# Weights of a hybrid attention and expert layer, laid out by the host as contiguous chunks of 1 MB

## The chip, the core and the metric

The kernel runs on one core of a Trainium2 chip. Its time is the time on the device, in microseconds (us), as the median of several runs. Matrix products run on TensorE (PE in the profile; PEld is its load of the stationary operand), elementwise work on VectorE (DVE) and ScalarE (ACT), a little on GpSimd (POOL). SyncE (SP) issues the loads, and 16 DMA engines carry them from HBM into SBUF, whose 128 partitions are the rows of every tile.

## What is computed

One decoder layer over 256 tokens of width 1024, in float32, with 256 memory tokens:

```python
proj = einsum('bsd,de->bse', rmsnorm(x, attn_norm_g), w_in)   # 1024 x 2320: three groups of heads
o_gla  = silu(gla_r) * rmsnorm(gla_chunked(q, k, v, forget_gate))
o_moba = moba_attention(qnorm(q), knorm(k), v, alibi_slopes)  # one block of 256: causal softmax
o_mem  = memory_attention(qnorm(q), *split(rmsnorm(mem) @ w_mem_kv))
x = x + concat(o_gla, o_moba, o_mem) @ w_out
h = rmsnorm(x, ffn_norm_g)
# experts: best of 4 groups, best 2 of its 8 experts; 32 experts of width 512
x = x + sum(gate[e] * ((silu(h @ w_gate[e]) * (h @ w_up[e])) @ w_down[e]) for e in chosen)
```

The projections w_in, w_mem_kv and w_out have some 16 MB, the weights of the 32 experts 192 MB (1 MB is 1,048,576 bytes where chunks are meant).

## The kernel before

All weights go through buffers of 1 MB, 128 partitions of 8 KB: a ring of 21 (`RING`), of which the attention part keeps some for its own data, and two more (`LATE`) later. A chunk of weights fills one buffer and is one DMA, issued by SP in the helper `chunk` (L93). The program's order of loads is the order on SP's queue; a load waits until the products that read its buffer's former contents are done.

**Attention part.** `load_chunk` loads 16 chunks: 512 columns of a projection by half of its eight k-tiles, so a partition gets four rows of 512 columns. They are issued in the order of the list `loads`, among small loads (gains, biases, router weights). The work on them follows one long list, `order`, in which every engine's instructions stand in fixed order: `w` splits a k-tile of weights in two float32r parts (ACT and DVE), `mm` multiplies.

**Experts.** `batch` runs over eight batches of four experts, each expert with 32 slots for tokens. A batch takes 24 chunks: four steps c of w_gate and w_up, each in two halves of two experts (`wNg`, `wNu` in the profile, N the batch), then eight chunks of w_down (`wNd`). A gate or up chunk has two k-rows of 512 columns for each of two experts: the k-rows of a partition are neighbours in HBM, since row d = 8 p + i of an expert lies on partition p. A down chunk has a row of 1024 columns for each of two experts. The last batch's down chunks are cut by columns, in order that output can leave earlier: four of 512 columns for one expert each, then four of 256 columns for two experts. Products: `pgate` and `pup` (L988), `pdn` (L1001, or L51 in the last batch, where a helper issues them), `acc` and `pc_b` for adding gated outputs to their tokens, `pg_b` for gathering tokens.

`prefetch(n)` puts the next n loads on SP's queue; `batch` calls it until the chunk that it needs is issued. Before batch 2 the kernel issues 20 loads ahead, then enters a loop over overflowing experts (`overflow`, L1086), which has no turns when, as here, no expert gets more than 32 tokens:

```python
for b in range(NB):
    if b == 1:
        overflow_blocks()
    if b == 2:
        prefetch(RING - 1)
        overflow()
    batch(b, final=(b == NB - 1))
```

Of the kernel before, what the change touches and what calls it, by code (L numbers as in the profile page):

```python
# [8 lines left out]
F32 = mybir.dt.float32  # L9
# [10 lines left out]
T = 256            # tokens  # L20
NT = T // P        # token tiles
D = 1024
KD = D // P        # k-tiles over the model width: row d = 128 * i + p, or 8 * p + i for the experts
FF = 512
KF = FF // P       # k-tiles over the expert width
NE = 32            # experts
EB = 4             # experts of one batch, one column group of the tensor engine each
C = 32             # slots of an expert in a batch
NB = NE // EB
NBLK = 16          # most blocks of 128 that assignments past slot C can fill  # L30
EPS = 1e-6
BIG = 1e30
RING = 21          # buffers of 1 MB: weight chunks in flight, and what the attention part keeps
LATE = 2           # more of them, once the attention part is done
H4 = 4             # heads of each group
SLOPES = [2.0 ** (-8.0 * (h + 1) / H4) for h in range(H4)]


class InOrder:
    """An engine whose instructions are issued in the order of the program."""  # L40
# [16 lines left out]
def layer(tc, x, mem, attn_norm_g, mem_norm_g, w_in, w_gla_gk, b_gla_gk, gla_out_norm_g,  # L57
          moba_q_norm_g, moba_k_norm_g, w_mem_kv, mem_q_norm_g, mem_k_norm_g, w_out,
          ffn_norm_g, w_router_group, b_router_group, w_router_expert, b_router_expert,
          w_gate, w_up, w_down, out):  # L60
    nc = tc.nc
    with ExitStack() as ctx:
# [5 lines left out]
        # in the order in which others want the space  # L68
# [18 lines left out]
        def chunk(src, name, shape, v=None):  # L87
            v = slot(name) if v is None else v
            if len(shape) == 2:
                v = v.rearrange("p (a b) -> p a b", a=shape[0])  # L90
            else:
                v = v.rearrange("p (a b c) -> p a b c", a=shape[0], b=shape[1])
            load(out=v, in_=src)  # L93
            return v

        # ---------------------------------------------------------------- loads and constants
# [5 lines left out]
        # what the attention part keeps, in buffers that hold weights later  # L102
# [17 lines left out]
        # gains and biases, as rows of 128 at first  # L120
# [6 lines left out]
        wkv = w_mem_kv[0].rearrange("(i p) e -> p i e", p=P)  # L127
        wo = w_out[0].rearrange("(i p) e -> p i e", p=P)
        columns = {"o": (wo, 0), "qk": (win, 0), "v": (win, 512), "r": (win, 1024), "mb": (win, 1552), "e": (win, 2064), "kv": (wkv, 0)}
        chunks = {}  # L130

        def load_chunk(name, h):
            """512 columns of a projection, half of its k-tiles; the output projection has columns twice that."""
            src, c = columns[name]
            c += 512 * (h // 2)
            chunks[name, h] = chunk(src[:, 4 * (h % 2):4 * (h % 2) + 4, c:c + 512], f"w_{name}{h}", (4, 512))
# [3 lines left out]
        # router weights (rows d = 512 * q + 4 * p + j) and bias; columns 4..7 pad the group logits to the 8 that max  # L140
        # takes
# [10 lines left out]
        def load_small(what):  # L152
# [11 lines left out]
            elif what == "qk gains":  # L164
                # for both heads of a pair
# [38 lines left out]
        # ---------------------------------------------------------------- attention part  # L204
# [8 lines left out]
        def split(src, hi, lo):  # L213
            """src as the sum of two float32r parts, exactly; products of them in three passes have float32's
            accuracy."""
            act.copy(hi, src)
            dve.tensor_tensor(lo, src, hi.bitcast(F32), op=ALU.subtract)
# [6 lines left out]
        def norm(src, r, name):  # L224
            """1 / rms of rows."""
            junk = work.tile([P, D], BF16, name="junk_" + name, tag="w2")
            ss = small.tile([P, 1], F32, name="ss_" + name, tag="ss")
            act.activation(junk, src, AF.Square, accum_out=ss)
            rstd_of(ss, 1, D, name, r)

        def norm_T(xh, t, q, dst, name):
            """Half of the columns, transposed and split: dst[part][q, i, token]."""
# [5 lines left out]
        def head_norm(ps, rx, n, name):  # L238
            """QK-norm, without the gains, of the n heads of 64 in ps times rx."""
# [10 lines left out]
        def heads_T(qn, t, n, g0, dst, name):  # L250
            """With the gains, transposed by head pairs into dst."""
# [16 lines left out]
        def softmax(sc, n, name, rl=None):  # L268
            """Softmax over the n keys of each head (sc: by head parity, [P, head pair, n])."""
# [22 lines left out]
        def softmax_T(ex, n, name):  # L292
            """Transposed: [key, key tile, head, query]."""
# [19 lines left out]
        # ---- the normalised rows  # L313
# [10 lines left out]
        def constants(what):  # L324
# [5 lines left out]
            elif what == "rel":  # L330
                # distance i - j of query i of the last tile to key j, huge where the key is later
# [3 lines left out]
            elif what == "amask":  # L335
                # key j (partition) of the same 64-chunk as query i and not later
# [7 lines left out]
        def more_constants():  # L344
# [3 lines left out]
            # strictly earlier tokens, and all tokens  # L348
# [17 lines left out]
        # ---- the projections in pieces: a k-tile of 512 columns  # L366
        weights, banks, passed = {}, {}, {}

        def w(name, n):
            """Splits the weights of piece n, with the gains of the norm before them."""  # L370
# [10 lines left out]
        def sums(name, n):  # L381
            """The bank, and whether this is the first, or the last, of the eight k-tiles that it sums."""
# [6 lines left out]
        def mm(name, n, t):  # L389
            """Piece n's products: rows of token tile t times 512 columns; for qk transposed, feature tiles 2 t and  # L390
            2 t + 1 by tokens; for the output projection, k-tile n % 8 of the mixed heads times columns of half n // 8."""
# [17 lines left out]
        # ---- what goes on between the pieces  # L409
        # MoBA and memory  # L410
# [19 lines left out]
        def go(key, f, *args):  # L430
            """The next part of a computation that goes on over several pieces; state keeps what it yields."""
# [44 lines left out]
        def rx_T(part):  # L476
            """The tokens' 1 / rms along the columns."""
# [36 lines left out]
        # GLA  # L514
# [4 lines left out]
        def lr_proj():  # L519
# [4 lines left out]
            # the sums over both parts of the weights, which the next product adds  # L524
# [53 lines left out]
        def inside():  # L578
            """Inside a chunk: masked products of queries and keys, transposed."""
# [11 lines left out]
        def states(part):  # L591
            """The states before chunks 1..3: products, then sums."""
# [70 lines left out]
        # ---- the last of the output projection, residual, FFN norm, router logits  # L663
# [101 lines left out]
        # ---- routing: top-1 group, top-2 experts in it  # L765
# [28 lines left out]
        # place of each assignment in its expert's list (from 1; 0 where the expert isn't chosen), and the  # L794
        # one-hot rows of the first batch
# [20 lines left out]
        def keep_warm(n):  # L816
            """Products that nobody reads: the array's clock halves when it idles."""
# [22 lines left out]
        # gate weight: softmax of the group, times softmax of the two chosen logits  # L840
# [20 lines left out]
        # ---------------------------------------------------------------- experts  # L861
        def gather(oh, name):
            """xg[p, i, slot]: normalised rows of the slots, transposed."""
# [26 lines left out]
        def spread(ohg, name):  # L890
            """One-hot rows with the gate weights, transposed: sT[slot, token]."""
# [9 lines left out]
        def combine(sT, pdn, name, half, first=False, last=False):  # L901
            """Adds the gated expert outputs of half the columns to their tokens' sums."""
# [6 lines left out]
        def combine_last(sT, pdn, name, cols):  # L909
            """Adds the gated expert outputs of the columns from cols on to their tokens."""  # L910
# [9 lines left out]
        def batch_onehot(b):  # L920
            """oh[token, expert and slot] of the batch's experts."""
# [10 lines left out]
        wg_v = w_gate[0].rearrange("e (p i) f -> p e i f", i=KD)  # L932
        wu_v = w_up[0].rearrange("e (p i) f -> p e i f", i=KD)
        wd_v = w_down[0].rearrange("e (i p) n -> p e i n", p=P)
        tiles = {}
        loads = []
        for b in range(NB):
            es = [slice(EB * b + 2 * h, EB * b + 2 * h + 2) for h in range(2)]
            for c in range(4):
                for kind, w in (("g", wg_v), ("u", wu_v)):  # L940
                    for h in range(2):
                        loads.append(((b, kind, c, h), w[:, es[h], 2 * c:2 * c + 2], (2, 2, FF)))
            if b < NB - 1:
                for c in range(KF):
                    for h in range(2):
                        loads.append(((b, "d", c, h), wd_v[:, es[h], c], (2, D)))
            else:
                for e in range(EB):
                    loads.append(((b, "d", 0, e), wd_v[:, EB * b + e, :, 0:512], (KF, 512)))
                for c in (1, 2):  # L950
                    for h in range(2):
                        n = 256 * (c + 1)
                        loads.append(((b, "d", c, h), wd_v.rearrange("p e i n -> p (e i) n")
                                      [:, KF * (EB * b + 2 * h):KF * (EB * b + 2 * h + 2), n:n + 256], (2 * KF, 256)))
# [11 lines left out]
        def batch(b, final=False):  # L966
# [5 lines left out]
            if final:  # L972
                # the sums so far; the last pieces are added one by one
# [32 lines left out]
            else:  # L1006
                prefetch(len(loads))

                # the columns in three pieces
# [3 lines left out]
                def down(c, part):  # L1013
                    """The products with half of the piece's weights, in the order in which they arrive."""
# [22 lines left out]
        def overflow_blocks():  # L1037
            """Lists the blocks of 128 for what doesn't fit in the C slots of an expert."""
# [121 lines left out]
```

## Time and profile before

| | |
|---|---|
| timed runs | 602.98 us median of 3 (602.48 to 603.61) |
| span of the profiled execution, first to last instruction | 602.5 us |
| median of the timed runs less that span | 0.5 us |
| TensorE products, busy | 468.2 us (78%) |
| VectorE, ScalarE, GpSimd, busy | 144.4, 111.1, 34.6 us |
| moved by DMA | 222.02 MB in 69898 packets, 369 GB/s over the span |
| mean granted clock of TensorE | 0.95 |

The profile is of one execution; its times run from the span's start. MB and GB are decimal in it. A DMA packet is one contiguous piece that one of the 16 engines carries, or the few bytes that signal the end of a load. The DMA share is the mean busy share of the 16 engines; packets overlap a little, so it can pass 1. A granted clock of 1.00 is the full 2.4 GHz of TensorE, 0.50 is 1.2 GHz.

### The profile page before, as it was taken

Reading aid. Unit: us, or ns where it says so; the run is one execution under the profiler, and the core shown is the slowest. Engines: PE = TensorE matmul, PEld = TensorE weight load, DVE = VectorE, ACT = ScalarE, POOL = GpSimd, SP = SyncE. Lnnn points to the kernel's source line nnn. Section 1 sums busy time; section 2 is a strip of 40 time slices with the busy share of each in tenths; the row PEclk is TensorE's granted clock in tenths of the full one; section 3 lists DMA queues with packets and bytes.
Section 4 is the critical chain, followed back from the end, with each engine's and each line's share of the span. In section 5 each row is a group of like instructions: output and inputs, shape, how many; then the busy total and the mean of one; then the engine's idle time right before and its main releaser. Section 6 shows DMA issues by size and latency. Waiting matters only on the chain.

```text
span 602.5 us, 6837 instructions
## 1 busy us (share of the span) xinstructions
PE 468.2 (78%) x2695; PEld 242.8 (40%) x2695; DVE 144.4 (24%) x316; ACT 111.1 (18%) x217; POOL 34.6 (6%) x76
## 2 busy tenths in 40 slices
PE   5999999999999850029997975698559855985577
PEld 4896777886444210024363521252116210621013
DVE  2769877756127000001010010001000100020002
ACT  5676667642010000000100010001000100010000
POOL 1323130101000000000000000000000000000001
PEclk9999999999998995559999999999999999999979
DMA  8899937696999999959999999999999999999995
GB/s 283 328 386 280 394 117 275 227 389 256 407 410 410 408 410 408 410 230 391 410 409 408 410 408 410 409 409 409 408 410 409 410 408 409 409 410 410 403 369 184
DMA packets 69898, 222.02 MB, mean 369 GB/s; under 512 B 7412, under 2 KB 11815, under 8 KB 69863
## 3 DMA queue, kind: packets, MB, share of 16 engines
q1 hardware_dynamic: 69462, 220.63, 94.5%
q0 software_dynamic: 256, 0.79, 0.4%
q8 instruction: 22, 0.36, 0.2%
q10 hardware_dynamic: 144, 0.13, 0.1%
q14 instruction: 14, 0.11, 0.0%
HBM read 220.49 MB, written 1.05 MB: 368 GB/s over the span
## 4 chain that ended last, share of the span: by engine, by line
DMA 34%; PE 19%; SPq 1%; DVE 1%; issue 0%; ACT 0%; DVEq 0%; ACTq 0%
DMA w4u<-in_w_up_dram 6%; DMA w5u<-in_w_up_dram 6%; DMA w6u<-in_w_up_dram 6%; PE pdn L1001 5%; PE pg_b L872 5%; DMA w6d<-in_w_down_dram 3%; DMA w3d<-in_w_down_dram 3%; PE pup L988 3%; DMA w3u<-in_w_up_dram 3%; DMA w7g<-in_w_gate_dram 3%; DMA w7d<-in_w_down_dram 2%; PE pdn L51 2%; PE pgate L988 2%; SPq L93 1%; PE acc L906 1%; PE pc_b L51 1%
## 5 line engine op out<-in xcount | busy, mean ns | idle before, releaser
L872 PE MATMUL pg_b<-ohs_b,x 128*128 128x128 f32 x224 | 57.2, 410 | 46.6 <-DVE ohs_b L866 45.9
L872 PEld LDWEIGHTS pg_b<-ohs_b,x 128*128 128x128 f32 x224 | 55.3, 334 | 55.8 <-DVE ohs_b L866 46.7
L882 DVE TENSOR_TENSOR sg_b<-sg_b,pup 128x512 f32<-128x512 f32 x8 | 5.5, 688 | 197.2 <-PE pup L988 197.2
L881 ACT ACTIVATE sg_b<-pgate 128x512 f32<-128x512 f32 x8 | 4.8, 597 | 169.8 <-PE pgate L988 169.8
L875 DVE TENSOR_TENSOR xg_b<-pg_b,g_ffn 128x512 f32<-128x512 f32 x14 | 9.3, 689 | 106.9 <-PE pdn L1001 80.6
L906 PE MATMUL acc<-y_b,sT_b 128*128 128x512 f32 x56 | 27.6, 615 | 2.8 <-ACT y_b L904 2.8
L904 ACT COPY y_b<-pdn 128x512 f32<-128x512 f32 x14 | 8.2, 586 | 112.7 <-PE pdn L1001 97.1
L929 POOL TENSOR_TENSOR oh<-oh,gates 128x256 f32<-128x256 f32 x8 | 4.9, 617 | 331.1 <-DVE ohs_b L866 321.1
L51 PE MATMUL p_o<-o_hi,memT 128*128 128x512 f32 x64 | 20.6, 403 | 0.0
L896 ACT COPY sT_b<-pst_b 128x256 f32<-128x256 f32 x8 | 3.0, 374 | 86.9 <-PE pst_b L894 78.6
L923 DVE TENSOR_TENSOR oh<-iota_s,posm 128x256 f32<-128x256 f32 x7 | 3.0, 422 | 66.1 <-SPq L1086 63.6
L51 PE MATMUL pdn<-w7d,hT_b 128*32 128x256 f32 (+1 forms) x96 | 15.2, 553 | 3.4 <-DMA w7d<-in_w_down_dram 2.8
L988 PE MATMUL pup<-w7u,xg_b 128*32 128x512 f32 x64 | 11.8, 601 | 7.5 <-DMA w7u<-in_w_up_dram 7.5
L988 PE MATMUL pup<-w4u,xg_b 128*32 128x512 f32 x64 | 11.8, 601 | 7.5 <-DMA w4u<-in_w_up_dram 7.5
L988 PE MATMUL pup<-w5u,xg_b 128*32 128x512 f32 x64 | 11.8, 601 | 7.5 <-DMA w5u<-in_w_up_dram 7.5
L988 PE MATMUL pup<-w6u,xg_b 128*32 128x512 f32 x64 | 11.8, 601 | 7.4 <-DMA w6u<-in_w_up_dram 7.4
L906 PEld LDWEIGHTS acc<-y_b,sT_b 128*128 128x128 f32 x56 | 9.5, 190 | 17.1 <-ACT y_b L904 10.4
L988 PE MATMUL pgate<-w6g,xg_b 128*32 128x512 f32 x64 | 10.8, 600 | 6.5 <-DMA w6g<-in_w_gate_dram 6.5
L988 PE MATMUL pgate<-w7g,xg_b 128*32 128x512 f32 x64 | 10.8, 600 | 6.5 <-DMA w7g<-in_w_gate_dram 6.5
L988 PE MATMUL pgate<-w4g,xg_b 128*32 128x512 f32 x64 | 10.8, 600 | 6.5 <-DMA w4g<-in_w_gate_dram 6.5
L988 PE MATMUL pgate<-w5g,xg_b 128*32 128x512 f32 x64 | 10.8, 600 | 6.5 <-DMA w5g<-in_w_gate_dram 6.5
L51 PE MATMUL p_mb<-mb_hi,hT 128*128 128x512 f32 x32 | 12.3, 473 | 1.0 <-ACT mb_hi L51 1.0
(322 smaller groups left out, 767.4 us busy)
## 6 DMA issues: line engine op xcount, KB each, us to landing
w0g<-in_w_gate_dram SPq DMA_DIRECT2D x8, 1024.0 KB
w0u<-in_w_up_dram SPq DMA_DIRECT2D x8, 1024.0 KB
w0d<-in_w_down_dram SPq DMA_DIRECT2D x8, 1024.0 KB
w1g<-in_w_gate_dram SPq DMA_DIRECT2D x8, 1024.0 KB
w1u<-in_w_up_dram SPq DMA_DIRECT2D x8, 1024.0 KB
w1d<-in_w_down_dram SPq DMA_DIRECT2D x8, 1024.0 KB
w2g<-in_w_gate_dram SPq DMA_DIRECT2D x8, 1024.0 KB
w2u<-in_w_up_dram SPq DMA_DIRECT2D x8, 1024.0 KB
```

Source lines behind the costliest of these rows:

```text
L51: r = getattr(self.engine, name)(*args, **kwargs)
L93: load(out=v, in_=src)
L872: nc.tensor.matmul(pgs[q][:, j], x2_i[:, t, 4 * q + j], ohs[:, t], start=(t == 0 and j == 0), stop=(t == NT - 1), skip_group_check=True)
L875: nc.vector.tensor_tensor(xg[:, 4 * q:4 * q + 4], pgs[q], g_ffn[:, 4 * q:4 * q + 4].unsqueeze(2).to_broadcast([P, 4, P]), op=ALU.mult)
L881: nc.scalar.activation(sg, pg, AF.Silu)
L882: nc.vector.tensor_tensor(sg, sg, pu, op=ALU.mult)
L896: nc.scalar.copy(sT, ps)
L904: nc.scalar.copy(y, pdn)
L906: nc.tensor.matmul(acc[t][half], sT[:, P * t:P * t + P], y, start=first, stop=last, skip_group_check=True)
L929: nc.gpsimd.tensor_tensor(oh, oh, gates[:, :, EB * b:EB * b + EB].unsqueeze(3).to_broadcast([P, NT, EB, C]), op=ALU.mult)
L988: nc.tensor.matmul(ps[s], xg[:, i, s], tiles[(b, kind, c, e // 2)][:, e % 2, ii], start=(i == 0), stop=(i == KD - 1))
L1001: nc.tensor.matmul(pdn[half][s], hT2[:, c, s], tiles[(b, "d", c, e // 2)][:, e % 2, 512 * half:512 * half + 512], start=(c == 0), stop=(c ...
```

## The change

The host builds two more inputs before the launch. `attn_pack` holds the 16 chunks of the attention part, `moe_pack` the 192 chunks of the experts in the order of loading; each chunk is stored as 128 partitions of 2048 floats, exactly as its buffer holds it. A load of a chunk then reads 1 MB of consecutive addresses, 8 KB a partition in one piece, where it read four pieces of 2 KB (attention), two of 4 KB (experts), four of 2 KB or eight of 1 KB (the last batch's down chunks). The weights in their old layout are still inputs: the low-rank gate columns and the overflow loop read them. The core of the diff (comments are taken out elsewhere, which moves line numbers):

```diff
+ATTN_CHUNKS = [(name, h) for name in ("mb", "qk", "e", "v", "r", "kv") for h in range(2)] + [("o", h) for h in range(4)]
+def moe_chunks():
+    out = []
+    for b in range(NB):
+        out += [((b, kind, c, h), (2, 2, FF)) for c in range(4) for kind in "gu" for h in range(2)]
+        if b < NB - 1:
+            out += [((b, "d", c, h), (2, D)) for c in range(KF) for h in range(2)]
+        else:
+            out += [((b, "d", 0, e), (KF, 512)) for e in range(EB)]
+            out += [((b, "d", c, h), (2 * KF, 256)) for c in (1, 2) for h in range(2)]
+    return out
...
         def chunk(src, name, shape, v=None):
             v = slot(name) if v is None else v
+            load(out=v, in_=src)
             if len(shape) == 2:
                 v = v.rearrange("p (a b) -> p a b", a=shape[0])
             else:
                 v = v.rearrange("p (a b c) -> p a b c", a=shape[0], b=shape[1])
-            load(out=v, in_=src)
             return v
...
         def load_chunk(name, h):
-            src, c = columns[name]
-            c += 512 * (h // 2)
-            chunks[name, h] = chunk(src[:, 4 * (h % 2):4 * (h % 2) + 4, c:c + 512], f"w_{name}{h}", (4, 512))
+            chunks[name, h] = chunk(attn_pack[ATTN_CHUNKS.index((name, h))], f"w_{name}{h}", (4, 512))
...
-        loads = []
-        for b in range(NB):
-            es = [slice(EB * b + 2 * h, EB * b + 2 * h + 2) for h in range(2)]
-            for c in range(4):
-                for kind, w in (("g", wg_v), ("u", wu_v)):
-                    for h in range(2):
-                        loads.append(((b, kind, c, h), w[:, es[h], 2 * c:2 * c + 2], (2, 2, FF)))
...
+        loads = [(key, moe_pack[n], shape) for n, (key, shape) in enumerate(moe_chunks())]
...
+def packed(w_in, w_mem_kv, w_out, w_gate, w_up, w_down):
...
+    attn = np.empty((len(ATTN_CHUNKS), P, 2048), f)
+    moe = np.empty((len(todo), P, 2048), f)
+    for n, ((b, kind, c, h), shape) in enumerate(todo):
+        e = slice(EB * b + 2 * h, EB * b + 2 * h + 2)
+        if kind in up:
+            part = up[kind][e, :, 2 * c:2 * c + 2].transpose(1, 0, 2, 3)
...
+        moe[n] = part.reshape(P, 2048)
+    return attn, moe
```

## Rows read from the trace of the kernel before

**Rows 1.** Busy time by stretch: engines (instructions), granted clock, DMA share, GB/s
```profile
core 0: us, PE busy (x) PEld busy (x) DVE busy (x) ACT busy (x) POOL busy (x), PEclk, DMA share, GB/s
...
146.20:147.50 1.30, 1.30 (x16) 0.39 (x12) 0.35 (x2) 0.88 (x6) 0.00 (x0) 1.00 0.00 0
147.50:265.60 118.10, 67.94 (x444) 28.15 (x436) 19.52 (x44) 6.74 (x11) 1.23 (x2) 0.81 1.01 400
265.60:272.00 6.40, 4.56 (x19) 4.56 (x20) 0.91 (x3) 0.00 (x0) 0.62 (x1) 0.50 0.22 70
272.00:571.00 299.00, 234.27 (x1323) 90.38 (x1322) 18.33 (x36) 14.62 (x27) 3.09 (x5) 1.00 1.03 408
571.00:582.00 11.00, 6.53 (x22) 1.26 (x22) 0.69 (x1) 0.59 (x1) 0.00 (x0) 0.91 1.06 381
```

**Rows 2.** The chain of waits in order of time: start us, us, what
```profile
401.82 5.27 PE pdn L1001 x40
...
408.83 18.72 DMA w5u<-in_w_up_dram
...
568.71 14.10 DMA w7d<-in_w_down_dram
...
582.85 6.49 PE pdn L51 x40
589.33 1.91 PE pc_b L51 x4
591.25 2.75 PE pdn L51 x32
594.00 1.06 PE pc_b L51 x4
595.06 1.88 PE pdn L51 x16
```

**Rows 3.** TensorE's waits, 266 to 583 us: us in total, times, longest us
```profile
PE pup L988 <- DMA w5u<-in_w_up_dram: 7.5, 7, 1.5
...
PE pgate L988 <- DMA w5g<-in_w_gate_dram: 6.5, 6, 1.5
```

**Rows 4.** SP's issues around the loop: start us, us, line, load, count
```profile
244.96 4.88 SPq L93 DMA_DIRECT2D w2d<-in_w_down_dram  x2
...
269.71 8.12 SPq L93 DMA_DIRECT2D w2d<-in_w_down_dram  x4
277.87 1.67 SPq L93 DMA_DIRECT2D w3g<-in_w_gate_dram  x2
```

**Rows 5.** SP's waits, 235 to 275 us
```profile
SPq L1086 <- SPq L1086: 15.4, 7, 2.6
```

**Rows 6.** DMA traffic, 300 to 560 us (4 KB pieces); then queue: packets, MB, share
```profile
DMA packets 27552, 106.36 MB, mean 409 GB/s; under 512 B 1616, under 2 KB 1616, under 8 KB 27540
...
q1 hardware_dynamic: 27540, 106.19, 102.5%
```

**Rows 7.** DMA traffic, 32 to 44 us (2 KB pieces)
```profile
DMA packets 2325, 4.64 MB, mean 387 GB/s; under 512 B 65, under 2 KB 65, under 8 KB 2323
```

**Rows 8.** DMA traffic, 583 to 590.5 us (1 KB pieces)
```profile
DMA packets 2586, 2.61 MB, mean 348 GB/s; under 512 B 38, under 2 KB 2586, under 8 KB 2586
```

**Rows 9.** One instruction fetch of 8 KB each: 99.0 to 99.4, 144.2 to 144.7 us
```profile
q14 instruction: 1, 0.01, 4.8%
...
q14 instruction: 1, 0.01, 3.9%
```

**Rows 10.** One instruction fetch of 16 KB, 138.4 to 139.4 us
```profile
q8 instruction: 1, 0.02, 5.9%
```

**Rows 11.** SP's issues, 147 to 148 us
```profile
147.34 0.37 SPq L93 DMA_DIRECT2D w0d<-in_w_down_dram  x1
147.80 0.42 SPq L93 DMA_DIRECT2D w1g<-in_w_gate_dram  x1
```

**Rows 12.** DMA traffic of SP's loads, 147.3 to 265.5 us
```profile
q1 hardware_dynamic: 12238, 47.19, 100.4%
```

**Rows 13.** DMA traffic of SP's loads, 269.7 to 571 us
```profile
q1 hardware_dynamic: 31865, 122.27, 102.1%
```

**Rows 14.** Busy time by stretch in the last batch
```profile
583.00:585.00 2.00, 2.00 (x12) 0.45 (x12) 0.00 (x0) 0.00 (x0) 0.00 (x0) 0.50 1.10 347
```

**Rows 15.** Waits for loads, 0 to 75 us
```profile
PE pt_x L48 <- DMA x<-in_x_dram: 4.2, 1, 4.2
...
ACT mb_hi L51 <- DMA w_mb<-in_w_in_dram: 2.2, 1, 2.2
```

More of the change, by code (lines that the diff above doesn't have):

```diff
@@ L59, in layer @@
           ffn_norm_g, w_router_group, b_router_group, w_router_expert, b_router_expert,
-          w_gate, w_up, w_down, out):
+          w_gate, w_up, w_down, attn_pack, moe_pack, out):
     nc = tc.nc
@@ L125, in layer @@
         g_qk, gno, bgk = gain_cols[:, 16:20], gain_cols[:, 20:21], gain_cols[:, 21:23]
-        wkv = w_mem_kv[0].rearrange("(i p) e -> p i e", p=P)
-        wo = w_out[0].rearrange("(i p) e -> p i e", p=P)
-        columns = {"o": (wo, 0), "qk": (win, 0), "v": (win, 512), "r": (win, 1024), "mb": (win, 1552), "e": (win, 2064), "kv": (wkv, 0)}
         chunks = {}
         def load_chunk(name, h):
-            src, c = columns[name]
-            c += 512 * (h // 2)
-            chunks[name, h] = chunk(src[:, 4 * (h % 2):4 * (h % 2) + 4, c:c + 512], f"w_{name}{h}", (4, 512))
+            chunks[name, h] = chunk(attn_pack[ATTN_CHUNKS.index((name, h))], f"w_{name}{h}", (4, 512))
         x2 = keep.tile([P, NT, D], F32, name="x2")
@@ L930, in batch_gates @@
                                     op=ALU.mult)
-        wg_v = w_gate[0].rearrange("e (p i) f -> p e i f", i=KD)
-        wu_v = w_up[0].rearrange("e (p i) f -> p e i f", i=KD)
-        wd_v = w_down[0].rearrange("e (i p) n -> p e i n", p=P)
         tiles = {}
-        loads = []
-        for b in range(NB):
-            es = [slice(EB * b + 2 * h, EB * b + 2 * h + 2) for h in range(2)]
-            for c in range(4):
-                for kind, w in (("g", wg_v), ("u", wu_v)):
-                    for h in range(2):
-                        loads.append(((b, kind, c, h), w[:, es[h], 2 * c:2 * c + 2], (2, 2, FF)))
[L943 to L954, printed above, removed]
+        loads = [(key, moe_pack[n], shape) for n, (key, shape) in enumerate(moe_chunks())]
         todo = iter(enumerate(loads))
@@ L1142 @@
         'w_gate', 'w_up', 'w_down']
+def packed(w_in, w_mem_kv, w_out, w_gate, w_up, w_down):
+    f = np.float32
+    attn = np.empty((len(ATTN_CHUNKS), P, 2048), f)
+    columns = {"o": (w_out, 0), "qk": (w_in, 0), "v": (w_in, 512), "r": (w_in, 1024), "mb": (w_in, 1552),
+               "e": (w_in, 2064), "kv": (w_mem_kv, 0)}
+    for n, (name, h) in enumerate(ATTN_CHUNKS):
+        src, c = columns[name]
+        c += 512 * (h // 2)
+        part = src[0].reshape(KD, P, -1)[4 * (h % 2):4 * (h % 2) + 4, :, c:c + 512]
+        attn[n] = part.transpose(1, 0, 2).reshape(P, 2048)
+    up = {"g": w_gate[0].reshape(NE, P, KD, FF), "u": w_up[0].reshape(NE, P, KD, FF)}
+    down = w_down[0].reshape(NE, KF, P, D)
+    todo = moe_chunks()
+    moe = np.empty((len(todo), P, 2048), f)
[3 more added lines that the diff above has]
+            part = up[kind][e, :, 2 * c:2 * c + 2].transpose(1, 0, 2, 3)
+        elif shape == (2, D):
+            part = down[e, c].transpose(1, 0, 2)
+        elif shape == (KF, 512):
+            part = down[EB * b + h, :, :, 0:512].transpose(1, 0, 2)
+        else:
+            part = down[e, :, :, 256 * (c + 1):256 * (c + 2)].transpose(2, 0, 1, 3)
+        moe[n] = part.reshape(P, 2048)
+    return attn, moe
 def kernel(**inputs):
@@ L1154 @@
         args.append(nc.dram_tensor(f"in_{name}_dram", a.shape, mybir.dt.from_np(a.dtype), kind="ExternalInput").ap())
+    packs = packed(*(np.asarray(inputs[name]) for name in ("w_in", "w_mem_kv", "w_out", "w_gate", "w_up", "w_down")))
+    for name, a in zip(("attn_pack", "moe_pack"), packs):
+        arrays[f"in_{name}_dram"] = a
+        args.append(nc.dram_tensor(f"in_{name}_dram", a.shape, F32, kind="ExternalInput").ap())
     args.append(nc.dram_tensor("out_0_dram", (1, T, D), F32, kind="ExternalOutput").ap())
```

## The prediction

> **What bounds the kernel now.** I read the stretches first: the span cut where the transfer rate changes. In [rows 1] the reader is to see that the DMA engines are idle for the last time just before 147.5 us (0 GB/s; up to there loads wait for the attention part to free buffers, not for bandwidth), that from 147.5 to 265.6 us they run full (share 1.01), that a hole of 70 GB/s follows for some 6 us, and that from 272 to 582 us they are full again (1.03, then 1.06). TensorE is busy 234 of the 299 us of the long stretch. So behind 147 us the kernel is a stream of weights with one hole and a tail; what a megabyte costs is what counts there.
>
> The chain of waits says the same: in [rows 2] it goes back from the end through products (582.85 us on) to w7d, and before that for some 18.7 us at a time to a w_up or w_gate load. The waits of TensorE [rows 3] are on those loads alone, 6 or 7 a batch, 1.5 us at most: it takes a chunk when it lands, and idles until the next.
>
> The hole is the entry of the overflow loop (L1086). SP issues w2d until 249.8 us, and issues again at 269.71 [rows 4]; between lie seven waits, up to 2.6 us each, 15.4 us in all [rows 5]. Those steps are one chunk's transfer long: SP waits there until every load under way has landed, chunk by chunk. Then come some 4 us of loop entry and the first load's latency. A faster stream drains sooner; it does not fill the hole.
>
> **The change part by part.** Numbers of instructions, issues, buffers, waits and bytes stay: each chunk is still one DMA of 1 MiB into the same buffer, from SP, in the same order. The packing is done by the host, outside the time. What changes is the length of one contiguous piece: 2 KB to 8 KB in the attention chunks, 4 KB to 8 KB in 184 of the expert chunks, and 2 KB (four) and 1 KB (four) to 8 KB in w7d.
>
> *Price of a piece.* Three stretches move pieces of one size with the engines full: 409 GB/s with 4 KB, 387 with 2 KB, 348 with 1 KB [rows 6 to 8]. With 16 engines a piece takes 16 x size / rate: 4096 B 160.2 ns, 2048 B 84.7 ns, 1024 B 47.1 ns. The steps are 75.5 ns for 2048 B and 37.6 ns for 1024 B, 36.9 and 36.7 ps per byte: a straight line, with about 9 ns that each piece costs whatever its size. On that line 8192 B take 160.2 + 4096 x 0.0369 = 311 ns. An engine carries 64 KB of a chunk: 16 pieces of 160.2 = 2.564 us now, 8 of 311.3 = 2.490 us then (421 GB/s): 0.074 us a chunk saved. From 2 KB (2.710 us) it is 0.220.
>
> No weight load of before has pieces of 8 KB, so the line has to be bounded. The nearest rows are the instruction fetches, which use the same engines: one packet of 8 KB has 4.8% of 16 engines in 0.4 us, that is 307 ns, another 3.9% in 0.5 us, 312 ns [rows 9]. With the rounding of the shares the first is 304 to 310 ns, the second 308 to 316. Against that stands a fetch of 16 KB: 5.9% in 1.0 us, 944 ns, where the line would give 613 [rows 10]. I take 311 from the line, since both packets of the very size lie on it; the bounds are 304 and 316 ns, 2.43 and 2.53 us a chunk; the 16 KB row is a rival, below.
>
> The Trainium skill, "DMA: Bandwidth & Descriptors", section Bandwidth, prices a load by the size of the whole DMA (1 MB at 341 GB/s, 16 MB at 425) and asks for 1 MiB or more; the size of the piece has no part in that table. By it the change, which keeps 1 MiB, would give 0; [rows 6 to 8] show 348 to 409 GB/s at one DMA size, so here the piece does matter.
>
> *Stretch before the hole.* At 147.34 us SP issues a w0d chunk into empty queues [rows 11]; from there to the drain 47.2 MB land [rows 12], 45 chunks. When it is issued hangs on TensorE's freeing of buffers and stays. 45 x 0.074 = 3.3 us.
>
> *Stretch behind it.* From 269.7 to 571 us 122.3 MB land [rows 13], 116 chunks of 4 KB pieces and a part of w7d: 116 x 0.074 = 8.6 us. One step gives back: after the loop three loads go out at once and the fourth only at about 277.5 us, when the first products have freed a buffer [rows 4]; the three end 0.2 us sooner and the engines wait 0.2 us longer. TensorE's cover: it has 65 us of 299 idle here, 13 us of each 61 us batch (24 x 2.564); a batch becomes 1.8 us shorter, so it does not become the bound.
>
> *The last batch.* The first four w7d chunks are all needed before the first column piece is done; the chain hangs on the fourth, until 582.8 us. 4 x 0.220 = 0.9 us. The four chunks of 1 KB pieces land 3.01 us apart now and 2.49 then, but products run without a gap from 582.85 to 596.9 us [rows 2], so this 2.1 us is hidden and I count 0. The granted clock is 0.50 at their start [rows 14], the 1.2 GHz level, after TensorE has waited for weights; I assume the same. At full clock the 40 products that take 6.49 us would take some 2 us less, by 40 wider products in 5.27 us in [rows 2]: a bound of 2 us on the good side.
>
> *Attention part.* The only waits on loads are 4.2 us for x, whose layout stays, and 2.2 us for w_mb [rows 15]. Two mb chunks ahead of that wait save at most 2 x 0.220 = 0.44 us, at least 0 if the other operand is as late; I take 0.2. The other twelve chunks are hidden by compute, and full buffers hold the first expert loads back anyway: 0.
>
> *Sum.* 3.3 + 8.6 - 0.2 + 0.9 + 0.2 = 12.8 us. The profiled span is 602.5 us, so 589.7. The median of the timed runs, 602.98, lies 0.5 above the span, which I take as what lies around it: 590.2 us.
>
> **The rivals.** *Pieces stay 4 KB.* If what turns a load into packets cuts at 4 KB, packets come out as in the 4 KB row, and only pieces that were shorter gain: 4 x (2.710 - 2.564) = 0.6 us and 0.2 in attention: 602.2 us, no change. For it: no weight packet of the trace is longer than 4 KB (106.19 MB in 27540 packets [rows 6], 1616 of them the few bytes that end a load). Against it: these engines do carry packets of 8 and 16 KB [rows 9, 10]; what becomes of a longer piece of a load, no row shows. The Trainium skill, same page, section "SWDGE vs HWDGE vs iDMA", calls a packet "≤4096 B preferably"; no weight load in this trace tests it.
>
> *Long pieces are slower.* If a piece beyond 4 KB goes at the 16 KB fetch's 57.6 ps per byte, it takes 472 ns, a chunk 3.78 us, 161 x 1.21 + 4 x 1.07 = 199 us more: about 802 us. It decides from 320 ns a piece on, twice the 4 KB price. For it: one size class of fetch. Against it: the 8 KB fetches at 307 and 312 ns, and that a fetch does not write where weights go.
>
> *More than the line.* With pieces at 304 ns, 161 x 0.132 + 4 x 0.28 = 22 us, and a tail that keeps its clock 2 us more: down to 578 us. 308 to 310 ns, where the two 8 KB rows overlap, give 586 to 589.
>
> **How the numbers follow.** Forecast (8 KB at 308 to 313 ns) 0.75: 586 to 592. Slower than the line but still a gain (up to 316 ns, 597 us) 0.06. Cut at 4 KB 0.09. Slower than before 0.05. Clearly more gain 0.05. A difference under 0.2% (1.2 us) can't be told from none here. Faster: 0.75 + 0.06 + 0.05 = 0.86; same: 0.09; slower: 0.05. The range 585 to 597 takes in the upper bound of a piece (316 ns) and leaves out the two rivals, 0.14, and most of the 0.05 below.
>
> **What would show it.** Right: weight packets half as many, some 421 GB/s in the long stretch, the TensorE waits still on w_up and w_gate, expert chunks 2.49 us apart; the drain ending 3 to 4 us earlier, the second issue phase with it; an unchanged hole of some 6 us; the last w7d wait over near 570 us; the tail behind it about 20 us as now. Wrong: 409 GB/s and as many packets (cut), a rate below 409 (long pieces dear), a full rate but a later start of the stream (attention held up), or TensorE without waits on weights (it has become the bound).

## The result, and the profile after

The changed kernel takes 589.48 us (median of 4 runs, 587.64 to 590.52) where the kernel before took 603.30 (4 runs): a ratio of 0.9768, 95% interval 0.9748 to 0.9788, 13.8 us less. Five more runs of it beside nine of before gave 588.87 against 603.54 and a ratio of 0.9758 (0.9745 to 0.9772). The forecast was 590.2 us.

The profiled execution was the quickest of its four: span 585.9 us, time 587.64. Its busy time by stretch, cut where the rate changes as in [rows 1] (engines with instructions, granted clock, DMA share, GB/s):

```profile
143.90:145.00 1.10, 1.10 (x16) 0.39 (x12) 0.14 (x1) 0.93 (x6) 0.00 (x0) 1.00 0.02 7
145.00:260.00 115.00, 66.57 (x448) 29.95 (x437) 19.71 (x45) 6.74 (x11) 1.24 (x2) 0.83 0.99 411
260.00:266.50 6.50, 4.72 (x20) 4.72 (x20) 0.91 (x3) 0.00 (x0) 0.62 (x1) 0.60 0.19 53
266.50:557.00 290.50, 237.78 (x1322) 91.06 (x1321) 18.31 (x36) 14.62 (x27) 3.08 (x5) 0.96 1.01 421
557.00:567.00 10.00, 5.55 (x22) 1.22 (x22) 0.69 (x1) 0.59 (x1) 0.00 (x0) 1.00 1.01 422
```

The shape is the same: engines idle until 145 us, a full stream, a hole, a full stream. The long stretch runs at 421 GB/s where it ran at 408, the last batch at 422 instead of 381, and the hole stays 6.5 us long.

The DMA traffic of 290 to 550 us shows why (packets, MB, rate; then the queue of SP's loads):

```profile
DMA packets 15025, 109.48 MB, mean 421 GB/s; under 512 B 1670, under 2 KB 1670, under 8 KB 1670
...
q1 hardware_dynamic: 15013, 109.31, 101.2%
```

But for the 1670 small packets, most of them the few bytes that end a load, none is under 8 KB: 109 MB in 13,355 packets, where [rows 6] had 25,936 for 106 MB. So the pieces are not cut at 4 KB.

TensorE's waits from 262 to 570 us, and SP's around the loop (us in total, times, longest):

```profile
PE pup L979 <- DMA w4u<-in_moe_pack_dram: 6.8, 7, 1.4
...
PE pgate L979 <- DMA w4g<-in_moe_pack_dram: 6.0, 6, 1.4
```

```profile
SPq L1077 <- SPq L1077: 18.6, 7, 3.8
SPq L106 <- DMA w2u<-in_moe_pack_dram: 8.4, 4, 2.1
```

TensorE still waits for gate and up chunks, a little less than in [rows 3]: the stream is still the bound. The drain in the loop (now L1077) is still there.

SP's issues at the start of the stream and behind the loop (start us, us, line, load, count), and the chain of waits at the end:

```profile
145.08 0.33 SPq L106 DMA_DIRECT2D w0d<-in_moe_pack_dram  x1
...
264.07 8.05 SPq L106 DMA_DIRECT2D w2d<-in_moe_pack_dram  x4
```

```profile
548.27 19.82 DMA w7d<-in_moe_pack_dram
...
568.13 4.50 PE pdn L68 x40
572.64 1.91 PE pc_b L68 x4
574.55 2.94 PE pdn L68 x30
577.49 1.06 PE pc_b L68 x4
578.55 1.88 PE pdn L68 x16
```

From the issue into the empty queue to the first issue behind the loop it is 264.07 - 145.08 = 118.99 us, before 269.71 - 147.34 = 122.37: 3.4 us less. From there to the 40 products of the last batch 304.06, before 313.14: 9.1 less. From these to the end of the span 17.8, before 19.6: 1.9 less. And the stream starts 2.3 us sooner. That is 16.6 us, the whole difference of the two spans. The first two numbers are the forecast's. The last two were not in it: as the experiments show, the start differs from one execution to the next, and the tail goes with the last batch's chunks.

The spans differ by more than the medians (16.6 against 13.8 us) because of which executions were profiled. In every run that lists both, the time is 1.7 to 1.8 us more than the span, so the profile of before, 602.5 us, belongs to an execution of some 604.2 us (an estimate), 0.9 above its median, and that of the changed kernel lies 1.8 below its own.

### The profile page after: what moved, and what is told of

It is laid out like the page before. It is cut to its first block, busy times and chain, and to the rows that moved or that the text cites. A ratio compares the mean times of both kernels' runs of the same rounds, so it can differ in the third digit from the quotient of the medians.

```text
span 585.9 us, 6837 instructions
## 1 busy us (share of the span) xinstructions
PE 465.7 (79%) x2695; PEld 244.0 (42%) x2695; DVE 144.3 (25%) x316; ACT 111.1 (19%) x217; POOL 35.3 (6%) x76
## 3 DMA queue, kind: packets, MB, share of 16 engines
HBM read 220.49 MB, written 1.05 MB: 378 GB/s over the span
## 4 chain that ended last, share of the span: by engine, by line
DMA 50%; PE 5%; issue 0%; DVE 0%; ACT 0%; SPq 0%; DVEq 0%; ACTq 0%
DMA w7u<-in_moe_pack_dram 7%; DMA w4u<-in_moe_pack_dram 7%; DMA w6u<-in_moe_pack_dram 7%; DMA w5u<-in_moe_pack_dram 7%; DMA w3u<-in_moe_pack_dram 6%; DMA w6d<-in_moe_pack_dram 3%; DMA w4d<-in_moe_pack_dram 3%; DMA w7d<-in_moe_pack_dram 3%; DMA w5d<-in_moe_pack_dram 3%; DMA w3d<-in_moe_pack_dram 3%; PE pdn L68 2%; PE pg_b L884 1%; PE pc_b L68 1%; PE pgate L979 1%; PE pup L979 0%
## 5 line engine op out<-in xcount | busy, mean ns | idle before, releaser
L979 PE MATMUL pup<-w7u,xg_b 128*32 128x512 f32 x64 | 15.0, 759 | 6.8 <-DMA w7u<-in_moe_pack_dram 6.8
L979 PE MATMUL pup<-w6u,xg_b 128*32 128x512 f32 x64 | 15.0, 760 | 6.7 <-DMA w6u<-in_moe_pack_dram 6.7
L979 PE MATMUL pup<-w4u,xg_b 128*32 128x512 f32 x64 | 13.5, 686 | 6.8 <-DMA w4u<-in_moe_pack_dram 6.8
L979 PE MATMUL pgate<-w5g,xg_b 128*32 128x512 f32 x64 | 12.4, 684 | 5.2 <-DMA w5g<-in_moe_pack_dram 5.2
L979 PE MATMUL pgate<-w4g,xg_b 128*32 128x512 f32 x64 | 10.8, 600 | 6.0 <-DMA w4g<-in_moe_pack_dram 6.0
L68 PE MATMUL pdn<-w7d,hT_b 128*32 128x256 f32 (+1 forms) x96 | 12.4, 453 | 3.5 <-DMA w7d<-in_moe_pack_dram 2.9
L68 PE MATMUL p_o<-o_lo,memT 128*128 128x512 f32 x32 | 12.6, 394 | 0.0
```

The source lines that it names most:

```text
L68: r = getattr(self.engine, name)(*args, **kwargs)
L979: nc.tensor.matmul(ps[s], xg[:, i, s], tiles[(b, kind, c, e // 2)][:, e % 2, ii], start=(i == 0), stop=(i == KD - 1))
```

## The experiments

**Which chunks matter.** Two kernels pack one half each. In the first the experts' loads go back to the old views, in the second the attention's. (Each diff is against the changed kernel; lines left out are marked by dots.)

```diff
 # attention only
-        loads = [(key, moe_pack[n], shape) for n, (key, shape) in enumerate(moe_chunks())]
...
+        loads = [(key, unpacked(key, shape), shape) for key, shape in moe_chunks()]
 # experts only
-            chunks[name, h] = chunk(attn_pack[ATTN_CHUNKS.index((name, h))], f"w_{name}{h}", (4, 512))
-            chunks[name, h] = chunk(attn_pack[ATTN_CHUNKS.index((name, h))], f"w_{name}{h}", (4, 512))
+            src, c = columns[name]
+            c += 512 * (h // 2)
+            chunks[name, h] = chunk(src[:, 4 * (h % 2):4 * (h % 2) + 4, c:c + 512], f"w_{name}{h}", (4, 512))
```

> Attention chunks packed, all expert chunks in their old layout. Theory (a piece costs 9 ns plus 36.9 ps a byte; only the expert stream is bound by it): the stretches keep 409 GB/s, the chunk at the last empty queue is issued at about 145 us as in the changed kernel (147.3 before), so 1 to 2.5 us are gained: 601 to 602.5 us. Rival (the packed attention chunks do nothing and the earlier start came with the packed expert chunks): the start stays at 147 us, 603 us. The 2.2 us at the start in the changed kernel came by 0.5 us from the landing of w_mb and the rest after TensorE's products went to full speed at 12.6 us instead of 16.9; if that is chance, the gain lies anywhere from 0.5 to 2.5 us.

> Expert chunks packed, attention chunks in their old layout. Theory: the stream runs at 421 GB/s, the start is that of before (147 us, TensorE at full speed from about 17 us), so the changed kernel's time plus 0.5 to 2.3 us: 590 to 592 us. Rival (packing both is needed, since attention and expert loads share the queue): clearly above 592 us. The first four chunks of the last batch land 2.49 us apart, and the tail behind the last wait for weights is 18 to 21 us, by the granted clock there.

Measured: attention alone 603.21 us beside 602.77 of before, ratio 1.0006 (0.9993 to 1.0019), nothing; my expectation of 1 to 2.5 us missed, and the stream started at 146.77 us, not at 145. Experts alone 589.51 us, ratio 0.9786 (0.9768 to 0.9804): all of the gain that can be told. Its long stretch:

```profile
DMA packets 15027, 109.50 MB, mean 421 GB/s; under 512 B 1670, under 2 KB 1670, under 8 KB 1670
```

**Length of a piece, or one run of addresses.** The change makes two things at once: pieces of 8 KB, and loads of 1 MB at consecutive addresses. The first kernel keeps the addresses and halves the pieces, the second keeps the pieces and lays them 1.5 MB apart.

```diff
 # four KB: a chunk is two halves of 128 x 4 KB
-            load(out=v, in_=src)
+            load(out=v.rearrange("p (a b) -> p a b", a=2), in_=src.rearrange("a p b -> p a b"))
...
-    moe = np.empty((len(todo), P, 2048), f)
+    moe = np.empty((len(todo), 2, P, 1024), f)
...
-        moe[n] = part.reshape(P, 2048)
+        moe[n] = part.reshape(P, 2, 1024).transpose(1, 0, 2)
 # far apart: all pieces of a partition in a row
-        loads = [(key, moe_pack[n], shape) for n, (key, shape) in enumerate(moe_chunks())]
+        loads = [(key, moe_pack[:, n], shape) for n, (key, shape) in enumerate(moe_chunks())]
...
-    moe = np.empty((len(todo), P, 2048), f)
+    moe = np.empty((P, len(todo), 2048), f)
...
-        moe[n] = part.reshape(P, 2048)
+        moe[:, n] = part.reshape(P, 2048)
```

> Attention as changed; each expert chunk is still 1 MB of consecutive addresses in the order of loading, but stored as two halves of 128 x 4 KB, so that a partition gets two pieces of 4 KB (in the last batch too). Theory (length of a piece): twice the packets, 409 GB/s in the long stretches, 161 x 0.074 us lost again and some 0.3 us in the last batch: 600 to 602.5 us. Rival (consecutive addresses of a whole load are what helps): 420 GB/s and more, 588 to 590 us.

> Pieces of 8 KB as changed, but the expert weights are stored partition by partition: the 128 pieces of a chunk lie 1.5 MB apart, and a partition's 192 pieces follow each other. Theory (length of a piece): 421 GB/s, 588 to 590.5 us, as the changed kernel. Rival (consecutive addresses help): the rate of before, 409 GB/s, about 601 us. Third: pieces at a wide pitch collide in HBM, and the stream falls below 409 GB/s, over 603 us.

Measured: 601.26 us with 4 KB pieces, ratio 0.9978 (0.9966 to 0.9990); 590.96 us with 8 KB pieces far apart, ratio 0.9819 (0.9787 to 0.9851). The traffic in the long stretch, first of the one, then of the other:

```profile
DMA packets 27562, 106.37 MB, mean 409 GB/s; under 512 B 1624, under 2 KB 1624, under 8 KB 27550
```

```profile
DMA packets 15025, 109.48 MB, mean 421 GB/s; under 512 B 1670, under 2 KB 1670, under 8 KB 1670
```

The rate goes with the piece alone. Consecutive addresses with 4 KB pieces give the rate of before; what is left of the gain, 1.5 us between the medians, is about the size of what its last batch shows, whose pieces grew from 1 and 2 KB to 4 (0.7 us up to the last products and 0.6 behind, table below). Scattered 8 KB pieces give the full rate. Their median is 1.5 us above the changed kernel's first one; their interval just overlaps that of its first comparison (up to 0.9788) and lies above that of its second (up to 0.9772). In the profile 0.9 to 1.0 us of it lies behind the hole (305.0 against 304.1 and 304.0 in the table below). Whether that is the layout stays open.

**The line itself.** A kernel of loads alone, from the packed expert weights. It leaves the layer out. In the code kb is the KB of a piece, mb the MB of a load, count the number of loads.

```diff
+for kb, mb, count in ((1, 1, 16), (2, 1, 24), (4, 1, 24), (8, 1, 24), (16, 2, 12), (32, 4, 6), (4, 4, 6), (8, 4, 6)):
+    a, per = 8 * mb // kb, 256 * kb
+    for k in range(count):
...
+        v = ring.tile([P, 8192], F32, name=name, tag="s")[:, 0:2048 * mb]
+        src = moe_pack[n:n + mb].rearrange("n p e -> (n p e)").rearrange("(a p b) -> p a b", a=a, p=P)
+        nc.sync.dma_start(out=v.rearrange("p (a b) -> p a b", a=a), in_=src)
...
```

> Loads alone; nothing of the layer is computed, and the output is a copy of x. From the packed expert weights, in turn: loads of 1 MB in pieces of 1, 2, 4 and 8 KB, loads of 2 MB in pieces of 16 KB, of 4 MB in pieces of 32 KB, then loads of 4 MB in pieces of 4 KB and of 8 KB. Theory (9 ns and 36.9 ps a byte for each piece, whatever the load): 348, 387, 409, 421, 428, 431, 409, 421 GB/s. Rival 1 (size of the load counts): the 4 MB loads with 4 and 8 KB pieces are clearly above 409 and 421. Rival 2 (long pieces are dear, as the fetch of 16 KB in 944 ns): 16 KB pieces at about 278 GB/s. Rival 3 (pieces longer than some size are cut): 16 and 32 KB as 8 KB.

Measured in one run, a stretch of 24 to 42 us inside each size, in the order of the expectation:

```profile
DMA packets 8295, 8.36 MB, mean 348 GB/s; under 512 B 128, under 2 KB 8295, under 8 KB 8295
...
DMA packets 8189, 16.25 MB, mean 387 GB/s; under 512 B 255, under 2 KB 255, under 8 KB 8189
...
DMA packets 4255, 16.39 MB, mean 410 GB/s; under 512 B 255, under 2 KB 255, under 8 KB 4255
...
DMA packets 2210, 16.02 MB, mean 422 GB/s; under 512 B 254, under 2 KB 254, under 8 KB 254
...
DMA packets 1122, 16.29 MB, mean 429 GB/s; under 512 B 128, under 2 KB 128, under 8 KB 128
...
DMA packets 550, 15.93 MB, mean 430 GB/s; under 512 B 64, under 2 KB 64, under 8 KB 64
...
DMA packets 4064, 16.38 MB, mean 410 GB/s; under 512 B 64, under 2 KB 64, under 8 KB 4064
...
DMA packets 2025, 16.06 MB, mean 423 GB/s; under 512 B 64, under 2 KB 64, under 8 KB 64
```

Expected were 348, 387, 409, 421, 428, 431, 409, 421: all eight hold within 2 GB/s. A load of 4 MB is no faster than one of 1 MB with the same pieces (410 and 410; 423 and 422), and pieces of 16 and 32 KB stay whole and on the line. The Trainium skill, "DMA: Bandwidth & Descriptors", section Bandwidth, prices by the size of the whole load, 341 GB/s at 1 MB; its table is of loads that GpSimd issues, while here SP issues them. With loads queued behind each other, as here, the measurement says that the piece decides: 348 to 422 GB/s at 1 MB.

**The last batch.** Everything packed but the eight down chunks of the last batch; and, in the same comparison, the changed kernel again.

```diff
+        loads = [(key, unpacked(key, shape) if key[:2] == (NB - 1, "d") else moe_pack[n], shape)
+                 for n, (key, shape) in enumerate(moe_chunks())]
```

> As changed, but the eight down chunks of the last batch in their old layout (pieces of 2 KB and 1 KB). Theory: the first four land 2.71 us apart instead of 2.49 and cost 0.9 us; the other four are hidden behind products unless these run at full clock, when the last chunk, 12 us behind the fourth instead of 10, holds the end up by up to 1 us: 0.9 to 2 us above the changed kernel, 590.4 to 591.5 us. Rival (the shorter tail of the changed kernel comes from these four chunks): 2 us or more above it. If the tail hangs on the clock alone, it is 20.5 us behind the last wait for weights where the products there start at granted clock 0.5, and 18 to 19.5 us at 1.0.

> The changed kernel once more. Theory: 421 GB/s, chunks 2.49 us apart, drain of the loop 3.3 us sooner after the start of the stretch, all as in its first profile. What can differ is where the granted clock falls: whether products reach full speed at 12.6 or about 17 us, and whether the 40 products behind the last wait take 4.5 or 6.5 us; 587.5 to 590.5 us by these. Rival: start and tail are fixed by the layout, both as in the first profile, and the time within 0.3 us of 587.6.

Measured: 591.52 us with the old last chunks, ratio 0.9805 (0.9792 to 0.9819); 588.87 us for the changed kernel, 0.9758. The eight chunks are worth 2.65 us, more than the 0.9 to 2 that I had said, and on the rival's side: most of it lies behind the last wait, in the tail. TensorE's products at the end (start us, us, count, wait before), old last chunks first, then the changed kernel again:

```profile
570.28 4.93 PE L68 MATMUL pdn<-w7d,hT_b 128*32 128x512 f32 x42 [1.78 <-DMA w7d<-in_w_down_dram]
...
579.25 1.92 PE L68 MATMUL pdn<-w7d,hT_b 128*32 128x256 f32 x16 [0.28 <-DMA w7d<-in_w_down_dram]
...
582.17 1.92 PE L68 MATMUL pdn<-w7d,hT_b 128*32 128x256 f32 x16
```

```profile
569.92 4.50 PE L68 MATMUL pdn<-w7d,hT_b 128*32 128x512 f32 x42 [1.45 <-DMA w7d<-in_moe_pack_dram]
...
576.26 3.01 PE L68 MATMUL pdn<-w7d,hT_b 128*32 128x256 f32 x32
...
580.27 1.92 PE L68 MATMUL pdn<-w7d,hT_b 128*32 128x256 f32 x16
```

(The list of products puts 42 together where the chain of waits has 40.) In both the 42 products run at full clock (granted clock 1.00; 4.9 and 4.5 us; in [rows 2] 6.5). With the old chunks the last 16 start 11.9 us behind the start of the 42, and one wait for weights shows between; with the new ones 10.4 us, without a wait.

The kernel with attention alone has the old last chunks too, and its 42 products run at a granted clock of 0.52 at first, near the 1.2 GHz level:

```profile
582.50:585.00 2.50, 2.42 (x12) 0.59 (x16) 0.00 (x0) 0.00 (x0) 0.00 (x0) 0.52 1.10 348
```

```profile
582.58 6.18 PE L68 MATMUL pdn<-w7d,hT_b 128*32 128x512 f32 x42 [1.68 <-DMA w7d<-in_w_down_dram]
...
594.66 1.92 PE L68 MATMUL pdn<-w7d,hT_b 128*32 128x256 f32 x16 [0.16 <-DMA w7d<-in_w_down_dram]
```

Its last 16 start 12.1 us behind, as in the kernel before, and wait 0.16 us for the last chunk. So with the old chunks the last 16 start 11.9 to 12.1 us behind at either clock, and four chunks at 3.01 us, the forecast's figure for them, take 12.0: their landing sets it.

The second look at the changed kernel shows what varies. It has the stretches of the first (see the table), but its stream starts at 146.67 us, not 145.08.

**What is left: longer pieces, no hole.** Two kernels take the theory further: buffers of 2 MB and expert loads with 16 KB pieces, and the changed kernel without the overflow loop, which leaves out the path for experts with more than 32 tokens.

```diff
 # sixteen KB
-RING = 21
-LATE = 2
+RING = 10
+LATE = 1
...
+                src = moe_pack[256 * n:256 * n + 256].rearrange("a e -> (a e)")
...
+                    load(out=v, in_=src.rearrange("(p f) -> p f", p=P))
 # no loop
-            if b == 2:
-                prefetch(RING - 1)
-                overflow()
```

> The step that the line of sizes points to: buffers of 2 MB (10 and one late) in place of 1 MB (21 and two), and expert loads of 2 MB with 16 KB a partition in one piece; attention chunks stay loads of 1 MB, two to a buffer, and the last batch's down chunks too. Theory: 428 GB/s in the long stretches, 2.45 us a megabyte instead of 2.49: 1.9 us less up to the drain, 5.0 us less behind it, 581 to 583 us. Rival: a buffer comes free, and a load counts as landed, only as 2 MB, so that the stream starts later (2 to 5 us), the first wait after the loop is longer, and the batch waits longer for its last load: as much as is gained, 586 to 590 us.

> The changed kernel without the overflow loop and the loads issued ahead of it: the path for experts with more than 32 tokens is left out (none has more here). Theory (behind 147 us a stream with one hole, and nothing else bounds it): no drain, the hole of 8.4 to 8.6 us goes, and TensorE keeps up: 580 to 581 us. Rival (TensorE, which works off 20 landed chunks after the drain, or the buffers, are the bound too): less than half of it gained, 585 us or more.

Measured: 586.74 us with 16 KB pieces, ratio 0.9719 (0.9706 to 0.9732), better than both kernels, but not by the 6.9 us hoped for, and inside the rival's 586 to 590. Its stream is as expected:

```profile
DMA packets 7339, 106.88 MB, mean 428 GB/s; under 512 B 814, under 2 KB 814, under 8 KB 814
```

Its issues at the start of the stream, and its last products:

```profile
146.89 0.33 SPq L966 DMA_DIRECT2D w0d<-in_moe_pack_dram  x1
149.99 0.33 SPq L966 DMA_DIRECT2D w1g<-in_moe_pack_dram  x1
```

```profile
566.57 7.44 PE L68 MATMUL pdn<-w7d,hT_b 128*32 128x512 f32 x42 [1.44 <-DMA w7d<-in_moe_pack_dram]
```

The 42 products begin 3.4 us sooner than in the second look at the changed kernel (569.92), and take 7.44 us instead of 4.50: the granted clock was 0.50 there, the 1.2 GHz level, up to 570 us:

```profile
566.50:570.00 3.50, 3.43 (x19) 0.81 (x23) 0.00 (x0) 0.00 (x0) 0.00 (x0) 0.50 1.02 424
```

So about half of the expected 6.9 us reached the last batch, where the clock took most of that in this profile; the median is 2.1 us below 588.87, measured in another comparison. The mean granted clock is lower in all five runs of this kernel (0.89 to 0.90, against 0.94 to 0.96 in the nine of the changed one); why was not tested.

For the other half, a count of what was still to be loaded tells more. SP's queue from the first issue into the empty queue to the 42 products, here (146.89 to 566.57 us) and in the second look at the changed kernel (146.67 to 569.92; packets, MB, share):

```profile
q1 hardware_dynamic: 12457, 175.69, 98.9%
...
q1 hardware_dynamic: 23914, 174.21, 99.2%
```

With 16 KB pieces 1.48 MB more was left, 3.5 us at 428 GB/s. That fits fewer and coarser buffers, which let the kernel load less ahead of the stream (its second load waits 3.1 us behind the first); no run changed the number of buffers alone.

Without the loop: 580.14 us, ratio 0.9623 (0.9606 to 0.9640). That is 8.7 us below 588.87 and 9.3 below 589.48, each from another comparison. For the size of the hole, the changed kernel's first profile around it; then, without the loop, SP's first issue into the empty queue and the 42 products:

```profile
258.00:278.00 20.00, 16.22 (x110) 10.40 (x114) 3.10 (x8) 0.37 (x1) 1.23 (x2) 0.82 0.67 267
```

```profile
145.05 0.33 SPq L106 DMA_DIRECT2D w0d<-in_moe_pack_dram  x1
...
560.39 4.50 PE L68 MATMUL pdn<-w7d,hT_b 128*32 128x512 f32 x42 [1.44 <-DMA w7d<-in_moe_pack_dram]
```

At 267 instead of 421 GB/s the 20 us lose 7.3 us (an estimate). Without the loop the way from the issue to the 42 products is 415.3 us, with it 423.05: 7.7 us less. Within these figures all of the hole is gained. The stretch that held the hole, 230 to 275 us, and the next:

```profile
230.00:275.00 45.00, 35.19 (x184) 14.40 (x182) 2.15 (x4) 2.18 (x4) 0.00 (x0) 1.00 1.01 421
275.00:550.00 275.00, 208.35 (x1072) 72.16 (x1072) 14.13 (x28) 12.07 (x23) 2.47 (x4) 0.98 1.01 421
```

## Why the prediction was right, point by point

The four stretches of the profiles with 1 MB chunks and the loop, in us, from rows like those shown for before and after (issue into the empty queue; to the first issue behind the loop; to the 42 products of the last batch; to the end of the span):

```
                       start   to loop's end   to last products   tail
before                 147.34      122.37           313.14        19.6
changed                145.08      118.99           304.06        17.8
changed, second look   146.67      119.30           303.95        17.8
attention only         146.77      122.57           313.24        19.6
experts only           146.82      119.31           304.18        17.8
four KB pieces         145.60      122.36           312.41        19.0
pieces far apart       146.56      119.33           305.00        17.8
last down chunks old   146.35      119.09           304.84        19.4
```

- *Price of a piece.* Right: 421 GB/s, and pieces are not cut. The line from three rates of before held up to 32 KB. The two bounds, 304 and 316 ns, were wider than needed; 16 x 8192 B at 422 GB/s is 311 ns, the value taken.
- *Stretch before the hole.* 3.3 us said, 3.4 measured; 3.0 to 3.4 in all runs with 8 KB pieces, 0 (within 0.2) in the two with 4 KB.
- *Hole.* It stays, and a faster stream does not fill it; without the loop its 7 to 8 us (by the profiles) were gained on top.
- *Stretch behind it.* 8.6 - 0.2 + 0.9 = 9.3 us said with the first four chunks of the last batch, 9.1 measured. With these four in the old layout 8.3 is left, so they are worth 0.8 to 0.9, as said.
- *Last batch, the four chunks of 1 KB pieces.* Here a term was mis-sized: I counted 0, because products ran without a gap in the profile of before. The first of those products ran at half clock, for 2 us longer, and so just covered the loads: the last 16 of them start when the last chunk has landed. I also assumed that this clock stays; in the changed kernel it was 1.00. At full clock the late chunks are the limit: 1.6 us of tail (19.4 against 17.8), and 2.65 us between the two medians together with the four chunks of 2 KB. With the old chunks the clock itself is worth only 0.2 us (19.6 against 19.4). I had named the clock as a bound of 2 us, but not that it is the cover of the loads. In the profile with 16 KB pieces, whose last chunks are as in the changed kernel, the products began at half clock again, and the tail was 20.4 us. This suggests, but does not show, that the forecast's 0 would have been near had the clock stayed. Why the products ran at full clock in five profiles with these chunks (4.50 us in both looks at the changed kernel, with experts alone, far apart and without the loop) and not in that one was not tested.
- *Attention part.* 0.2 us said; attention alone measured nothing. The first product on w_mb does start sooner where the attention chunks are packed (10.1 to 10.4 us against 10.7 and 10.8), but this does not reach the median. The 2.3 us by which the first profile's stream started sooner are not the layout's: the same kernel looked at again has 0.7. They go with the moment when TensorE's products first run at full speed. In the first look pairs of products are 1.05 us until 12.8 us and 0.62 then; in the second until 15.5, in the kernel before until 17.1; in the runs with 13 us the stream starts at 145.1 to 145.6, in those with 15.4 us and more at 146.3 to 147.3. The granted clock reads 1.00 in all these stretches (4 to 20 us), so it does not show the step, and why the step comes sooner in one execution than in another was not tested. (The prediction's "twelve" other chunks are fourteen.)
- *Rivals.* Cut at 4 KB: refuted by packets and rate. Long pieces dear like the fetch of 16 KB: refuted, weight pieces of 16 KB run at 429 GB/s, 611 ns each. The Trainium skill, "DMA: Bandwidth & Descriptors", section "SWDGE vs HWDGE vs iDMA", calls packets of 4096 B or less preferable, in a table on the descriptors that GpSimd builds; the profile's packets of 8 to 32 KB, from loads that SP issues, were faster here (422 to 430 GB/s against 410).
- *Sum.* 12.8 us said, 13.8 and 14.7 measured (603.30 less 589.48, 603.54 less 588.87). With 0 for attention and 1.6 for the four chunks of 1 KB pieces the sum is 14.2, so it is in part chance that the first comparison came within 1 us of the forecast. The 0.5 us that I took to lie around the span is 1.7 to 1.8 in every run that lists both; the profile of before was of a longer execution than the four timed ones. It cancels in the forecast, which comes to the median of before less 12.8.

## What to carry to other kernels

Where a queue of loads sets the time, take the rate of two or three sizes of contiguous piece from the same trace, draw the line, and read the gain of a new layout off it; for the rate, the run of addresses and the size of the load did not matter here, only the piece. Multiply by the chunks that the full stretches carry, not by all: what is loaded while buffers are short gained nothing here. And before a load is counted as hidden by products, look at the clock at which those products ran.

## What was not expected of the hardware

- With 4 KB pieces and a full queue an issue keeps SP for about 2.4 us (two in 4.88 us, [rows 4]); with 8 KB pieces it takes 0.33 us in the full stream too (0.327 to 0.328 for the eight w4g, which took 2.29 to 4.64 before), and SP waits for an earlier load instead (the 8.4 us in four waits above). The chain of waits then goes from a load to its issue in steps of 19.82 us, eight chunks of 2.48, as with eight loads under way. No run shows that this changed the time.
- The granted clock drops in the middle of the full stream, in pieces of a few us, in some executions: not in the profile of the kernel before (1.00 from 300 to 560 us), but in the changed kernel's, and as much in that of attention alone, whose expert loads are the old ones. The mean clock of a whole run was 0.91 to 0.96 in the kernel before and 0.94 to 0.96 in the changed one, so the new layout is not needed for it. Here are 15 us of the changed kernel, then 260 of attention alone; both have TensorE waiting for chunks again and again:

```profile
375.00:390.00 15.00, 12.42 (x44) 5.42 (x44) 0.69 (x1) 0.98 (x2) 0.00 (x0) 0.77 1.02 422
```

```profile
300.00:560.00 260.00, 211.54 (x1069) 78.67 (x1067) 15.43 (x30) 11.88 (x22) 2.47 (x4) 0.94 1.03 409
```

The stream hides it: the rates are 422 and 409 GB/s all the same.

- A fetch of instructions of 16 KB took 944 ns [rows 10], a weight piece of 16 KB 611 ns: this row for one kind of traffic was no price for the other.
